# Second FFN of a decoder trunk: weight-block sums for six up tiles made in HBM ahead, and the second up part wholly by seven block products

## The chip, the cores and the metric

The kernel runs on one core of one Trainium2 chip. The metric is device time in microseconds for one launch; lower is better. TensorE (PE) multiplies, VectorE (DVE) and ScalarE (ACT) do the elementwise work, GpSimd (POOL) does a little elementwise work and issues DMAs that add into HBM, SyncE (SP) issues nearly all loads.

## The reference

A two-layer decoder trunk on 512 positions of width 1024, all in float32. The part that matters here is the gated FFN that stands in both layers:

```python
def conv_ffn(xn, w_up, conv_w, conv_b, w_down):          # d = 1024, D_FF = 2816
    S = xn.shape[1]
    h = xn @ w_up                                         # 1024 -> 2 * 2816
    hp = jnp.pad(h, ((0, 0), (CONV_WIDTH - 1, 0), (0, 0)))
    c = conv_b + sum(hp[:, t:t + S] * conv_w[t] for t in range(CONV_WIDTH))
    g, u = jnp.split(c, 2, axis=-1)
    return (jax.nn.silu(g) * u) @ w_down
```

Layer 0 is a gMLP mixer, this FFN and a gated embedding; then one shared K/V projection; layer 1 is windowed attention, the FFN again and a gated embedding; a final RMSNorm ends it.

## The kernel before

**Splits.** Every float32 matrix product is made of three products of float32r parts: an operand is cast to float32r (`wh`, by ACT) and the remainder is taken (`wl`, by DVE), and PE adds high x high, high x low and low x high. So each weight block that PE uses has first cost one ACT cast and one DVE subtraction. They are made in `pump`, in pieces called units of up to 1024 columns, into four pairs of buffers (`WBUFS = 4`), so at most four units ahead of PE.

**Up tiles.** The up projection is cut into 22 tiles (index 0 to 21; "11th to 16th" are 10 to 15). Tile j makes 128 gate rows and the 128 line rows that belong to them. A plain tile (`up`) takes 8 blocks of the inner dimension, 2 halves and 3 products: 48 matmuls of 512 columns, and 2 units of weights. A tile in `UPS` is made by `woven_up`: the 2x2 block product with seven block multiplications instead of eight (Strassen's, in Winograd's form), each for 4 pairs of blocks: 7 x 4 x 3 = 84 matmuls of 256 columns. It needs sums of weight blocks. With the four blocks 0 to 3 of a pair, `weave` makes on DVE block 1 + block 0 and block 1 + block 3 (one instruction of 1024 columns, L163), then the next two sums from these (512 columns each, L164 and L165). The blocks and sums make three and a half units (three of 1024 columns and one of 512), each cast and subtracted in `pump`. After the products `woven_up` puts the two results together with two more DVE instructions (L812, 256 columns; L813, 512 columns) and five small ACT copies. Its output lies in SBUF: in the tiles `gate` and `line`, or, for the tiles in `ASIDE`, in a slot of the activations named `out`.

**After a tile**, `gated` applies the convolution (one ACT instruction and two DVE instructions of about 512 columns, L762, on each half), silu (ACT) and the product (DVE, L769). Two tiles that follow each other are one `Pair`, whose block sums and splits (L518 to L535, L312) feed the down projection.

**Parts.** The 22 tiles go in three parts (0 to 7, 8 to 15, 16 to 21), and the first tile of the next part is computed ahead of the down projection of the part before. The second part thus runs on PE as: tiles 9 to 15, then tile 16, then the down projection of tiles 8 to 15 in `woven_add` (PE tiles `dx` and `dy`, sums of weights in `weave` too), whose results GpSimd's queue adds into HBM (`saved<-head`, `saved<-tail`, L600). In the second part of both FFNs the tiles 9, 10, 12, 14 and 16 are woven and 11, 13 and 15 are plain.

**Loads.** `load` fetches one piece (one tile's weights, 1 MB) by one DMA on SP's queue into the next of three staging slots; a woven tile takes a second slot for its sums. A slot is free when the last split that reads it is done.

**Order.** Each engine works through its instructions in the order in which the scheduler of the framework left them. `behind(a, b)` only holds a after b in that order; it makes no wait.

Of the kernel before, what the change touches and what calls it, by code (L numbers as in the profile page):

```python
# [52 lines left out]
def tile_yoco(ctx: ExitStack, tc: tile.TileContext, t, out: bass.AP, out_b: bass.AP):  # L53
    nc = tc.nc
# [9 lines left out]
    dram = ctx.enter_context(tc.tile_pool(name="dram", bufs=1, space=bass.MemoryType.DRAM))  # L64
# [3 lines left out]
        return mmp.tile([P, S], F32, tag="mm", name=name)  # L68


    pieces, paired, woven, beside = [], set(), set(), set()

    def plan(ap_, n, cols, own=None):
# [23 lines left out]
    def plan_woven(w, n_chunks, k0, k1):  # L97

        for c in range(n_chunks):
            n = (k1 - k0) * P  # L100
            woven.add(len(pieces))
            pieces.append((w[c, :, k0 * 256 : k1 * 256], 2 * n, [(0, n)] * 3 + [(0, n // 2)], None))

    def plan_ups(l, j0, j1):
        for j in range(j0, j1):
            (plan_woven if j in UPS else plan_cols)(t["w_up"][l, j : j + 1], 1, *((0, KD) if j in UPS else (KD,)))

    def plan_ffn(l):
        plan(t["pT"][l], 2 * S, S, own=[(mp, "m4", "m5")])
# [33 lines left out]
    def behind(ins, front):  # L143

        tc.add_manual_dep(ins.ins, front.ins.name,
                          mybir.DependencyInfo(mybir.DependencyClass.NoSync, mybir.DependencyReason.DATA),
                          reason="order")

    def staged(name):
        tags = state["tags"]  # L150
        r = wp.tile([P, 2 * UNIT], F32, tag=f"r{tags[state['turn'] % len(tags)]}", bufs=1, name=name)
        state["turn"] += 1
        return r

    def weave(i, q):


        n = pieces[i][1] // 4
        g = raws[i][:, : 4 * n].rearrange("p (k b m) -> p b k m", b=4, m=P)
        if q == 0:  # L160
            s = sums[i] = staged(f"wsum{i}")[:, : 4 * n].rearrange("p (b k m) -> p b k m", b=4, m=P)
            k = n // P
            nc.vector.tensor_add(s[:, 0::3], g[:, 1:2].to_broadcast([P, 2, k, P]), g[:, 0::3])  # L163
            nc.vector.tensor_add(s[:, 2], s[:, 3], g[:, 0])  # L164
            nc.vector.tensor_add(s[:, 1], s[:, 2], g[:, 2])  # L165
        return (g[:, 0:3:2], sums[i][:, 2:4], sums[i][:, 0:2], g[:, 3:4])[q]

    def load(upto, queue=nc.sync):
        while state["raw"] < min(upto, len(pieces)):
            j = state["raw"]  # L170
            a, m = pieces[j][:2]
            r = raws[j - 1][:, UNIT:] if j in beside else staged(f"wraw{j}")
            ins = queue.dma_start(r[:, :m].rearrange("p (c m) -> p c m", c=2) if j in paired else r[:, :m], a)
            for front in state["sent"].pop(j, []):
                behind(ins, front)
            raws[j] = r
            state["raw"] += 1
# [145 lines left out]
    class Norm:  # L323
# [11 lines left out]
        def square(self, k, eng=None):  # L335
            sq = tp.tile([P, S], F32, tag="sq", name=f"{self.name}sq{k}")
            box["squared", k] = ins = nc.scalar.activation(sq, h[k], AF.Square)
            if self.acc is None:
                self.acc = sq
            else:  # L340
                acc = tp.tile([P, S], F32, tag="acc", name=f"{self.name}acc{k}")
                self.added = (eng or nc.gpsimd).tensor_add(acc, self.acc, sq)
                self.acc = acc
            return ins

# [99 lines left out]
        def rstd(self):  # L445

            r = tp.tile([P, S], F32, tag="rstd", name=f"{self.name}rstd")
            if self.line is not None:
                nc.gpsimd.dma_start(r, self.line.partition_broadcast(P))
            else:  # L450
                nc.scalar.copy(r, self.spread(0, S // 64))
            return r

    def inv_root(ms, name, scale=1.0, n=None):
        if n is None:
            n = ms.shape[1]
            ms = [(slice(None), ms)]
        m = const.tile([P, n], F32, tag=f"ms{n}", bufs=2, name=f"{name}m")
        for some, x in ms:
            box["m"] = nc.vector.tensor_scalar(m[some, :], x, scale, EPS, op0=ALU.mult, op1=ALU.add)  # L460
        r = const.tile([P, n], F32, tag=f"rt{n}", bufs=2, name=f"{name}rt")
        nc.gpsimd.tensor_tensor(r, m, minus_half[:, :n], op=ALU.pow)
        return r

    box = {}
# [264 lines left out]
    def ffn(l, norm, nxt):  # L730
# [4 lines left out]
            behind(nc.sync.dma_start(saved[k], h[k]), box["squared", k])  # L735

        def up(j, later=False):
            if j in UPS:
# [13 lines left out]
            return pss if later else gated(j, pss)  # L752
# [34 lines left out]
        def woven_up(j, later):  # L787

            product = products(ins)
            n = PAIRS * P  # L790
            chain, other = psum(f"ux{j}")[:, first], psum(f"uy{j}")
            if j in ASIDE:
                head, tail = couple(ASIDE[j], f"out{j}", F32)
# [18 lines left out]
            nc.vector.tensor_sub(tail[:, second], tail[:, second], side)  # L812
            nc.vector.tensor_add(head, head, other)  # L813
            return (head, tail) if later else gated(j, (head, tail))
# [91 lines left out]
    def ple(l, norm, nxt, pe):  # L906
        xs = norm.xs[0][0]
        rstd, held = None, []
        for c in range(4):
            parts = chunk(256, KD)  # L910
# [114 lines left out]
    edge = at.tile([P, PAIRS, 2, N], F32R, tag="vtl", name="edge")  # L1025
    us = [Pair(c, edge, f"us{c}", range(3 * PAIRS)) for c in range(PAIRS)]
    for c in range(4):
        parts = chunk(256, KD)
        ups = [psum(f"u{c}_{j}") for j in range(2)]
        for j in range(2):  # L1030
# [47 lines left out]
    for k in range(KD):  # L1078
        nm.split(k, 1)
        if k == 3:  # L1080
            nm.turn()
    rt = nm.begin(rows=2)

    state["tags"] = [0, 1]
    parts = chunk(256, KD)
# [1 line left out]
    mm3(qps[0], parts, xq, 0)  # L1087
    rstd = nm.rstd()
    mm3(qps[1], parts, xq, P)

    for j in range(2):
        kf = tp.tile([P, S], F32, tag="acc", name=f"kf{j}")
# [314 lines left out]
    r = [f"r{(state['turn'] + j) % 3}" for j in range(3)]  # L1407
# [229 lines left out]
```

## Time and profile before

| | us |
|---|---|
| median of 3 runs | 1100.43 (1099.83 to 1101.02) |
| the profiled execution's own time | 1100.39 |
| its span | 1098.7 |
| second FFN, tile 9 to the down projection of part two | 838.6 to 922.7 of the span |
| first FFN, the same stretch | 290.8 to 373.5 of the span |

The profile is of one execution; times inside it count from the span's start. 1.69 us of the execution's time lie outside the span. A busy PE in the profile is a PE without gaps between matmuls; the chain of waits tells what PE was held by, and the timeline of DVE when each split was ready. In the timeline an instruction's duration overlaps the next one's start by about 0.08 us, so what an instruction costs its engine is read from start to start.

### The profile page before, as it was taken

Reading aid. Unit: us, or ns where it says so; the run is one execution under the profiler, and the core shown is the slowest. Engines: PE = TensorE matmul, PEld = TensorE weight load, DVE = VectorE, ACT = ScalarE, POOL = GpSimd, SP = SyncE. Lnnn points to the kernel's source line nnn. Section 1 sums busy time; section 2 is a strip of 40 time slices with the busy share of each in tenths; the row PEclk is TensorE's granted clock in tenths of the full one; section 3 lists DMA queues with packets and bytes.
Section 4 is the critical chain, followed back from the end, with each engine's and each line's share of the span. In section 5 each row is a group of like instructions: output and inputs, shape, how many; then the busy total and the mean of one; then the engine's idle time right before and its main releaser. Section 6 shows DMA issues by size and latency. Waiting matters only on the chain.

```text
span 1098.7 us, 17476 instructions
## 1 busy us (share of the span) xinstructions
PE 1089.1 (99%) x6629; PEld 974.4 (89%) x6629; DVE 959.0 (87%) x1540; ACT 661.0 (60%) x1141; POOL 125.0 (11%) x192
## 2 busy tenths in 40 slices
PE   9999999999999999999999999999999999999997
PEld 7888988899998999988888887888999989999886
DVE  5588889999899989877988997799998999898887
ACT  5735666565676656655656775565655666567544
POOL 2200200000100010021114452000001000100200
PEclk9999999999999999999999999999999999999999
DMA  9621674125633267353234216441255333664534
GB/s 317 113 88 39 178 264 150 43 77 116 155 115 116 79 160 222 120 190 112 67 87 135 78 58 227 176 153 39 77 142 128 115 116 86 156 220 142 203 95 98
DMA packets 47508, 144.24 MB, mean 131 GB/s; under 512 B 13048, under 2 KB 18688, under 8 KB 36928
## 3 DMA queue, kind: packets, MB, share of 16 engines
q1 hardware_dynamic: 40560, 128.77, 35.6%
q0 software_dynamic: 5296, 9.70, 6.7%
q10 hardware_dynamic: 1568, 4.65, 1.1%
q8 instruction: 52, 0.85, 0.3%
q14 instruction: 32, 0.26, 0.1%
HBM read 116.89 MB, written 18.88 MB: 124 GB/s over the span
## 4 chain that ended last, share of the span: by engine, by line
PE 95%; DVE 2%; issue 1%; ACT 1%; DMA 0%; SPq 0%; POOLq 0%; POOL 0%; ACTq 0%
PE up L234 20%; PE ux L234 10%; PE dx L234 10%; PE uy L234 8%; PE dy L234 8%; PE d L234 6%; PE q L234 4%; PE gate L234 4%; PE u L234 4%; PE o L234 4%; PE up L750 2%; PE pv L1326 1%; PE v L244 1%; PE v L245 1%; PE v L246 1%; PE pin L234 1%
## 5 line engine op out<-in xcount | busy, mean ns | idle before, releaser
L204 DVE TENSOR_TENSOR wl<-wraw,wh 128x1024 fp32r<-128x1024 f32 (+2 forms) x198 | 217.3, 1102 | 42.8 <-ACT wh L203 41.9
L203 ACT CAST wh<-wraw 128x1024 fp32r<-128x1024 f32 (+2 forms) x197 | 182.8, 933 | 107.6 <-PE up L234 21.8
L203 ACT CAST wh<-wsum 128x1024 fp32r<-128x1024 f32 x84 | 88.3, 1052 | 62.7 <-issue 14.9
L204 DVE TENSOR_TENSOR wl<-wsum,wh 128x1024 fp32r<-128x1024 f32 x84 | 102.5, 1225 | 16.1 <-ACT wh L203 16.0
L762 DVE SCALAR_TENSOR_TENSOR c<-up,vec,c 128x511 f32<-128x511 f32 (+1 forms) x88 | 65.0, 744 | 2.4 <-ACT c L760 1.9
L234 PE MATMUL up<-nf10h,wh 128*128 128x512 f32 x160 | 62.3, 389 | 0.0
L234 PE MATMUL up<-nf00h,wh 128*128 128x512 f32 x160 | 62.3, 389 | 0.0
L234 PE MATMUL up<-nf10l,wh 128*128 128x512 f32 x160 | 62.3, 389 | 0.0
L234 PE MATMUL up<-nf00l,wh 128*128 128x512 f32 x160 | 62.3, 389 | 0.0
L234 PE MATMUL up<-nf00h,wl 128*128 128x512 f32 x160 | 62.1, 389 | 0.0
L234 PE MATMUL up<-nf10h,wl 128*128 128x512 f32 x160 | 62.0, 389 | 0.0
L600 POOL DMA_DIRECT2D saved<-head x16 | 13.9, 871 | 412.9 <-DVE head L720 412.9
L760 ACT ACTIVATE c<-up,vec 128x512 f32<-128x512 f32 x44 | 34.0, 777 | 31.8 <-PE up L234 26.6
L163 DVE TENSOR_TENSOR wsum<-wraw 128x1024 f32<-128x1024 f32 x42 | 51.2, 1220 | 0.6
L234 PE MATMUL ux<-t,wh 128*128 128x256 f32 x264 | 50.4, 283 | 0.0
L234 PEld LDWEIGHTS ux<-t,wh 128*128 128x128 f32 x264 | 41.2, 192 | 0.0
L234 PE MATMUL ux<-t,wl 128*128 128x256 f32 x132 | 37.4, 283 | 0.0
L234 PEld LDWEIGHTS up<-nf00h,wl 128*128 128x128 f32 x160 | 30.0, 188 | 6.2
L234 PEld LDWEIGHTS up<-nf10h,wl 128*128 128x128 f32 x160 | 30.0, 188 | 6.2
L234 PEld LDWEIGHTS up<-nf00l,wh 128*128 128x128 f32 x160 | 30.0, 188 | 6.2
L234 PEld LDWEIGHTS up<-nf10l,wh 128*128 128x128 f32 x160 | 30.0, 188 | 6.2
L234 PEld LDWEIGHTS up<-nf10h,wh 128*128 128x128 f32 x160 | 30.0, 188 | 6.0
(769 smaller groups left out, 3734.3 us busy)
## 6 DMA issues: line engine op xcount, KB each, us to landing
wraw<-in_w_up SPq DMA_DIRECT2D x44, 1024.0 KB, 5.6
wraw<-in_w_down SPq DMA_DIRECT2D x16, 1024.0 KB, 5.0
wraw<-in_w_gate SPq DMA_DIRECT2D x8, 1024.0 KB, 5.5
wraw<-in_w_down SPq DMA_DIRECT2D x8, 768.0 KB, 4.5
wraw<-in_w_u SPq DMA_DIRECT2D x4, 1024.0 KB, 9.4
wraw<-in_w_out SPq DMA_DIRECT2D x4, 1024.0 KB, 4.9
saved<-head POOLq DMA_DIRECT2D x16, 256.0 KB, 4.2
saved<-tail POOLq DMA_DIRECT2D x16, 256.0 KB, 4.1
```

The costliest lines, as they stand in the source:

```text
L163: nc.vector.tensor_add(s[:, 0::3], g[:, 1:2].to_broadcast([P, 2, k, P]), g[:, 0::3])
L203: cast = nc.scalar.copy(hi, src)
L204: state["split"] = splits[u] = cast, nc.vector.tensor_sub(low, src, hi.bitcast(F32))
L234: return [nc.tensor.matmul(ps, w, x, start=first and j == 0, stop=last and j == len(todo) - 1, skip_group_check=onto) for j, (w, x) in enu ...
L244: nc.tensor.matmul(ps, xh[:, s], wh[:, a:b], start=st, stop=False)
L245: nc.tensor.matmul(ps, xl[:, s], wh[:, a:b], start=False, stop=False)
L246: nc.tensor.matmul(ps, xh[:, s], wl[:, a:b], start=False, stop=en)
L600: box["onto"] = nc.gpsimd.dma_start(x, y, accum_op=ALU.add)
L750: nc.tensor.matmul(ps, w[:, off + s * P : off + (s + 1) * P], x, start=k == 0 and x is xh and w is wh, stop=k == KD - 1 and x is xl)
L760: nc.scalar.activation(c, ps, AF.Identity, bias=v("conv_b", l * 2 * NJ + col), scale=cw[2])
L762: ins = nc.vector.scalar_tensor_tensor(c[:, tap:], ps[:, : S - tap], cw[2 - tap], c[:, tap:], op0=ALU.mult, op1=ALU.add)
L1326: nc.tensor.matmul(ps, lhs, rhs, start=j == 0, stop=j == len(todo) - 1)
```

## The change

It touches the up tiles 10 to 15 of the second FFN.

1. **Plain to woven.** Tiles 11, 13 and 15 of the second FFN become woven, so that in its second part all of 9 to 16 are. Their outputs go to slots 7, 12 and 12 (`ASIDE`).
2. **Sums in HBM.** For tiles 10 to 15 of the second FFN `weave` makes no sums any more. They are made in HBM during the first FFN, in two batches (tiles 10 and 11, tiles 12 to 15). Each batch is six steps: SP copies block 1 twice into the sums' places; GpSimd's queue adds block 3 to the one and block 0 to the other; copies the first sum on; adds block 0; copies on; adds block 2. Rows are runs of 128 floats in the steps that read the weights. The steps are called at the first FFN's tiles 1, 2, 3 and 5 (first batch) and 9, 10, 11 and 13 (second batch); each is held in its queue's order behind the last load (SP) or behind the last instruction marked `box["onto"]` (GpSimd).
3. **Loads.** Such a tile is loaded by four DMAs on SP's queue into two slots (the blocks 0 and 2 and two sums into `wraw`, two sums and block 3 into `wsum`): 1.75 MB in place of 1 MB. Around the six tiles `flip` changes the order of two slots.

```diff
-UPS = (7, 8, 9, 10, 12, 14, 16, 17, 18, 20, 21)
-ASIDE = {7: 12, 9: 7, 17: 7, 20: 6}
+UPS = [(7, 8, 9, 10, 12, 14, 16, 17, 18, 20, 21), (7, 8, 9, 10, 11, 12, 13, 14, 15, 16, 17, 18, 20, 21)]
+ASIDE = [{7: 12, 9: 7, 17: 7, 20: 6}, {7: 12, 9: 7, 11: 7, 13: 12, 15: 12, 17: 7, 20: 6}]
+BATCHES = [
+    (1, 10, 12, [("up", 0, 1), ("up", 0, 2), ("up", 0, 3), ("up", 0, 3), ("up", 0, 5), ("up", 0, 5)]),
+    (1, 12, 16, [("up", 0, 9), ("up", 0, 10), ("up", 0, 11), ("up", 0, 11), ("up", 0, 13), ("up", 0, 13)]),
+]
...
+    def sums_ahead(l, j0, j1, keys):
+        n = KD // 2 * P
+        whole = dram.tile([(j1 - j0) * P, 4 * n], F32, name=f"sums{l}_{j0}")
+        w = t["w_up"][l, j0:j1].rearrange("j p (k b m) -> (j p) k b m", b=4, m=P)
+        s = {x: whole[:, i * n : (i + 1) * n].rearrange("r (k m) -> r k m", m=P) for i, x in enumerate((2, 3, 0, 1))}
...
+        def copy(x, y):
+            behind(nc.sync.dma_start(x, y), state["loaded"])
+        def onto(x, y):
+            behind(nc.gpsimd.dma_start(x, y, accum_op=ALU.add), box["onto"])
+        def then(x, y):
+            behind(nc.gpsimd.dma_start(s[x], s[y]), box["onto"])
+        steps = [lambda: [copy(s[x], w[:, :, 1]) for x in (3, 0)],
+                 lambda: [onto(s[x], w[:, :, x]) for x in (3, 0)],
+                 lambda: then(2, 3), lambda: onto(s[2], w[:, :, 0]),
+                 lambda: then(1, 2), lambda: onto(s[1], w[:, :, 2])]
...
@@ in weave
+        if i in summed:
+            a, c = raws[i]
+            return (a[:, : 2 * n].rearrange("p (k b m) -> p b k m", b=2, m=P),
+                    a[:, 2 * n :].rearrange("p (b k m) -> p b k m", b=2, m=P),
+                    c[:, : 2 * n].rearrange("p (b k m) -> p b k m", b=2, m=P),
+                    c[:, 2 * n : 3 * n].rearrange("p (b k m) -> p b k m", b=1, m=P))[q]
@@ in load
+            if j in summed:
+                n = m // 4
+                if j - 1 not in summed:
+                    flip()
+                x, y = raws[j] = staged(f"wraw{j}"), staged(f"wsum{j}")
+                for there, here in ((x[:, : 2 * n].rearrange("p (k m) -> p k m", m=P),
+                                     a.rearrange("p (k m) -> p k m", m=P)[:, 0::2]),
+                                    (x[:, 2 * n :], summed[j][:, : 2 * n]),
+                                    (y[:, : 2 * n], summed[j][:, 2 * n :]),
+                                    (y[:, 2 * n : 3 * n].rearrange("p (k m) -> p k m", m=P),
+                                     a.rearrange("p (k m) -> p k m", m=P)[:, 3::4])):
+                    state["loaded"] = queue.dma_start(there, here)
+                state["raw"] += 1
+                if j + 1 not in summed:
+                    flip()
+                continue
```

**What moves in the engines' order.** Three places. On **DVE**, around the end of tile 10 of the second FFN (`wl221` to `wl224` are splits of tiles 11 and 12, `line10` and `gate10` put tile 10's result together, `act1_0_2l` is a split of activations). Before:

```order
L204 TENSOR_TENSOR wl221_9150<-wraw85_9117,wh221_9149 128x1024
L312 TENSOR_TENSOR act1_0_2l_9072<-act1_0u_9073,act1_0_2h_9071 128x512
L163 TENSOR_TENSOR wsum86_9182<-wraw86_9178 128x2x512
L204 TENSOR_TENSOR wl222_9181<-wraw86_9178,wh222_9180 128x1024
L164 TENSOR_TENSOR wsum86_9182<-wsum86_9182,wraw86_9178 128x512
L812 TENSOR_TENSOR line10_9086<-line10_9086,side10_9087 128x256
L165 TENSOR_TENSOR wsum86_9182<-wsum86_9182,wraw86_9178 128x512
L813 TENSOR_TENSOR gate10_9085<-gate10_9085,uy10_9084 128x512
L204 TENSOR_TENSOR wl223_9219<-wsum86_9182,wh223_9218 128x1024
```

Now:

```order
L274 TENSOR_TENSOR wl221_9172<-wraw85_9135,wh221_9171 128x1024
L382 TENSOR_TENSOR act1_0_2l_9090<-act1_0u_9091,act1_0_2h_9089 128x512
L885 TENSOR_TENSOR line10_9104<-line10_9104,side10_9105 128x256
L886 TENSOR_TENSOR gate10_9103<-gate10_9103,uy10_9102 128x512
L274 TENSOR_TENSOR wl222_9201<-wsum85_9136,wh222_9200 128x1024
L274 TENSOR_TENSOR wl223_9240<-wsum85_9136,wh223_9239 128x512
L835 SCALAR_TENSOR_TENSOR c10_0_9219<-gate10_9103,vec_86,c10_0_9219 128x511
```

Tile 12's three sums are gone; tile 11 has four splits (`wl220` to `wl223`) where it had two, so `wl222` and `wl223`, before the first of tile 12, are now the last of tile 11.

On **DVE** again, the last rows before the first split of the down projection (`wl238` before, `wl244` now; `c15` and `a15` are tile 15's convolution and gate, `wsum91` the down projection's sums, `act1_3` the last pair). Before:

```order
L762 SCALAR_TENSOR_TENSOR c15_1_9715<-up15_1_9662,vec_84,c15_1_9715 128x511
L163 TENSOR_TENSOR wsum91_9777<-wraw91_9773 128x2x512
L762 SCALAR_TENSOR_TENSOR c15_1_9715<-up15_1_9662,vec_84,c15_1_9715 128x510
L164 TENSOR_TENSOR wsum91_9777<-wsum91_9777,wraw91_9773 128x512
L769 TENSOR_TENSOR a15_9719<-a15_9719,c15_1_9715 128x512
L165 TENSOR_TENSOR wsum91_9777<-wsum91_9777,wraw91_9773 128x512
L532 TENSOR_TENSOR act1_3t_9654<-a15_9719,a14_9650 128x256
L533 SCALAR_TENSOR_TENSOR act1_3u_9725<-act1_3t_9654,a15_9719 128x256
L312 TENSOR_TENSOR act1_3_0_9722<-a15_9719,act1_3_0_9722 128x512
L535 SCALAR_TENSOR_TENSOR act1_3u_9725<-act1_3u_9725,a15_9719 128x256
L204 TENSOR_TENSOR wl238_9776<-wraw91_9773,wh238_9775 128x1024
```

Now:

```order
L835 SCALAR_TENSOR_TENSOR c15_0_9905<-out15_9790,vec_86,c15_0_9905 128x510
L216 TENSOR_TENSOR wsum91_9967<-wraw91_9963 128x2x512
L842 TENSOR_TENSOR a15_9913<-a15_9913,c15_1_9909 128x512
L217 TENSOR_TENSOR wsum91_9967<-wsum91_9967,wraw91_9963 128x512
L604 TENSOR_TENSOR act1_3t_9785<-a15_9913,a14_9781 128x256
L605 SCALAR_TENSOR_TENSOR act1_3u_9919<-act1_3t_9785,a15_9913 128x256
L382 TENSOR_TENSOR act1_3_0_9916<-a15_9913,act1_3_0_9916 128x512
L607 SCALAR_TENSOR_TENSOR act1_3u_9919<-act1_3u_9919,a15_9913 128x256
L218 TENSOR_TENSOR wsum91_9967<-wsum91_9967,wraw91_9963 128x512
L382 TENSOR_TENSOR act1_3_1_9917<-act1_3t_9785,act1_3_1_9917 128x512
L382 TENSOR_TENSOR act1_3_2_9918<-act1_3u_9919,act1_3_2_9918 128x512
L274 TENSOR_TENSOR wl244_9966<-wraw91_9963,wh244_9965 128x1024
```

All three splits of the last pair now stand ahead of the first split of the down projection; before, two of them stood behind it. All four convolution instructions of tile 15 now come after that tile's last product; before, the two of its first half came earlier.

On **POOL**, between the first FFN's two down projections (`saved<-head` and `saved<-tail` are their results). Before:

```order
L600 DMA saved0_5_1548<-tail2_2805 128x512
L600 DMA saved0_6_1549<-head3_2923 128x512
L600 DMA saved0_7_1550<-tail3_2924 128x512
L600 DMA saved0_0_1543<-head0_3980 128x512
L600 DMA saved0_1_1544<-tail0_3981 128x512
```

Now:

```order
L672 DMA saved0_6_1551<-head3_2933 128x512
L672 DMA saved0_7_1552<-tail3_2934 128x512
L130 DMA sums1_12_85<-in_w_up 512x4x128 x2
L133 DMA sums1_12_85<-sums1_12_85 512x512
L130 DMA sums1_12_85<-in_w_up 512x4x128
L133 DMA sums1_12_85<-sums1_12_85 512x512
L130 DMA sums1_12_85<-in_w_up 512x4x128
L672 DMA saved0_0_1545<-head0_3998 128x512
L672 DMA saved0_1_1546<-tail0_3999 128x512
```

The second batch's six DMAs stand between the two down projections; from the third on, each waits for the one whose sum it reads. The first batch's six stand in the same way ahead of the first FFN's first down projection.

More of the change, by code (lines that the diff above doesn't have):

```diff
@@ L68, in psum, with behind @@
         return mmp.tile([P, S], F32, tag="mm", name=name)
+    def behind(ins, front):
+        tc.add_manual_dep(ins.ins, front.ins.name,
+                          mybir.DependencyInfo(mybir.DependencyClass.NoSync, mybir.DependencyReason.DATA),
+                          reason="order")
     pieces, paired, woven, beside = [], set(), set(), set()
@@ L102, in plan_woven, with come @@
             pieces.append((w[c, :, k0 * 256 : k1 * 256], 2 * n, [(0, n)] * 3 + [(0, n // 2)], None))
+    summed, far_sums, to_come = {}, {}, {}
+    def sums_ahead(l, j0, j1, keys):
[3 more added lines that the diff above has]
+        s = {x: whole[:, i * n : (i + 1) * n].rearrange("r (k m) -> r k m", m=P) for i, x in enumerate((2, 3, 0, 1))}
+        for j in range(j0, j1):
+            far_sums[l, j] = whole[(j - j0) * P : (j - j0 + 1) * P]
+        def copy(x, y):
[8 more added lines that the diff above has]
+                 lambda: then(1, 2), lambda: onto(s[1], w[:, :, 2])]
+        for key, step in zip(keys, steps):
+            to_come.setdefault(key, []).append(step)
+    def come(*key):
+        for step in to_come.pop(key, []):
+            step()
+    for batch in BATCHES:
+        sums_ahead(*batch)
     def plan_ups(l, j0, j1):
         for j in range(j0, j1):
-            (plan_woven if j in UPS else plan_cols)(t["w_up"][l, j : j + 1], 1, *((0, KD) if j in UPS else (KD,)))
+            if (l, j) in far_sums:
+                summed[len(pieces)] = far_sums[l, j]
+            (plan_woven if j in UPS[l] else plan_cols)(t["w_up"][l, j : j + 1], 1,
+                                                       *((0, KD) if j in UPS[l] else (KD,)))
     def plan_ffn(l):
@@ L141, in tile_yoco, with flip @@
     state = {"raw": 0, "unit": 0, "next": 0, "tags": [0, 1, 2], "turn": 2, "pt": 0, "sent": {}}
[L143 to L147, printed above, removed]
+    def flip():
+        tags, i = state["tags"], state["turn"] + 1
+        a, c = i % 3, (i + 1) % 3
+        tags[a], tags[c] = tags[c], tags[a]
     def staged(name):
@@ L448, in rstd @@
             if self.line is not None:
-                nc.gpsimd.dma_start(r, self.line.partition_broadcast(P))
+                box["onto"] = nc.gpsimd.dma_start(r, self.line.partition_broadcast(P))
             else:
@@ L737, in up @@
         def up(j, later=False):
-            if j in UPS:
+            come("up", l, j)
+            if j in UPS[l]:
                 return woven_up(j, later)
@@ L791, in woven_up @@
             chain, other = psum(f"ux{j}")[:, first], psum(f"uy{j}")
-            if j in ASIDE:
-                head, tail = couple(ASIDE[j], f"out{j}", F32)
+            if j in ASIDE[l]:
+                head, tail = couple(ASIDE[l][j], f"out{j}", F32)
             else:
@@ L909, in ple @@
         for c in range(4):
+            come("gate", l, c)
             parts = chunk(256, KD)
@@ L1027, in tile_yoco @@
     for c in range(4):
+        come("u", c)
         parts = chunk(256, KD)
@@ L1082, in tile_yoco @@
     rt = nm.begin(rows=2)
+    come("k")
     state["tags"] = [0, 1]
@@ L1089, in tile_yoco @@
     mm3(qps[1], parts, xq, P)
+    come("q")
     for j in range(2):
@@ L1406, in tile_yoco @@
     parts2 = chunk(S, KD, ahead=2 * WBUFS)
-    r = [f"r{(state['turn'] + j) % 3}" for j in range(3)]
+    r = [f"r{state['tags'][(state['turn'] + j) % 3]}" for j in range(3)]
     turned_b = squares(wp, r[0], "turned_b")
```

5 lines of the change are left out of this document (4 added, 1 removed).

## The prediction

> **What bounds the kernel now.** The page first. PE is busy for 99% of the span and is 95% of the chain that ended last; DVE is busy for 87%.
>
> ```profile
> span 1098.7 us, 17476 instructions
> PE 1089.1 (99%) x6629; PEld 974.4 (89%) x6629; DVE 959.0 (87%) x1540; ACT 661.0 (60%) x1141; POOL 125.0 (11%) x192
> PE 95%; DVE 2%; issue 1%; ACT 1%; DMA 0%; SPq 0%; POOLq 0%; POOL 0%; ACTq 0%
> ```
>
> Shares are means, so next the busy times by stretch: the second FFN's part two, a piece of it from the first split of tile 11 to that of the down projection, and the first FFN's part two.
>
> ```profile
> core 0: us, PE busy (x) PEld busy (x) DVE busy (x) ACT busy (x) POOL busy (x), PEclk, DMA share, GB/s
> 838.60:922.70 84.10, 84.10 (x570) 77.67 (x569) 80.98 (x118) 55.43 (x89) 1.34 (x2) 1.00 0.34 108
> 853.75:920.24 66.49, 66.49 (x424) 60.16 (x424) 64.81 (x97) 43.55 (x69) 0.00 (x0) 1.00 0.30 104
> 290.80:373.50 82.70, 82.70 (x559) 76.27 (x558) 79.58 (x116) 54.40 (x89) 1.32 (x2) 1.00 0.34 110
> ```
>
> PE has no gap at all in the stretch that the change shortens, but DVE is busy for 81.0 of its 84.1 us. PE sets the end by a small margin; the question is what DVE does when PE gets shorter.
>
> **PE: three tiles become shorter.** The chain in order of time gives both kinds of tile:
>
> ```profile
> 869.97 1.43 PE ux L234 x12
> ...
> 880.03 10.91 PE up L234 x48
> 890.94 1.43 PE ux L234 x12
> ```
>
> Tile 12 (woven) starts at 869.97 and tile 13 (plain) at 880.03: 10.06 us. Tile 13 takes 10.91. A tile that changes kind saves 0.85 us, three save 2.55 us. That is all that PE can gain, since it has no gap there to close.
>
> **DVE: what goes and what comes.** One stretch of its timeline, tile 10's end, prices each kind of instruction from start to start:
>
> ```profile
> 861.71 0.41 DVE L812 TENSOR_TENSOR line<-line,side 128x256 f32<-128x256 f32 x1
> 862.05 0.68 DVE L165 TENSOR_TENSOR wsum<-wsum,wraw 128x512 f32<-128x512 f32 x1
> 862.65 0.68 DVE L813 TENSOR_TENSOR gate<-gate,uy 128x512 f32<-128x512 f32 x1
> 863.25 1.21 DVE L204 TENSOR_TENSOR wl<-wsum,wh 128x1024 fp32r<-128x1024 f32 x1
> 864.39 0.75 DVE L762 SCALAR_TENSOR_TENSOR c<-gate,vec,c 128x511 f32<-128x511 f32 x1
> 865.06 0.74 DVE L762 SCALAR_TENSOR_TENSOR c<-line,vec,c 128x511 f32<-128x511 f32 x1
> ```
>
> 256 columns cost 0.34 us, 512 cost 0.60, 1024 cost 1.14, a convolution step 0.67. The sums of a tile (1024, 512, 512) are 2.34 us; tiles 10, 12 and 14 lose them: -7.0. A tile that becomes woven has one more split of 1024 and one of 512 (1.74) and two instructions to put it together (0.94): 2.68, three times +8.0. So DVE has 1.0 us more to do while PE has 2.55 us less, against some 3 us in which DVE is idle in that stretch. All of those would have to be usable.
>
> **Where the two meet.** PE's next fixed point is the down projection's first use of a remainder, and DVE makes that remainder at the end of a long run without free choice of order:
>
> ```profile
> 847.44 0.69 DVE L813 TENSOR_TENSOR out9h<-out9h,uy 128x512 f32<-128x512 f32 x1 [0.47 <-PE uy L234]
> ...
> 853.75 1.22 DVE L204 TENSOR_TENSOR wl<-wraw,wh 128x1024 fp32r<-128x1024 f32 x1
> ...
> 871.37 1.52 DVE L762 SCALAR_TENSOR_TENSOR c<-up,vec,c 128x511 f32<-128x511 f32 x2
> 872.99 0.69 DVE L769 TENSOR_TENSOR a<-a,c 128x512 f32<-128x512 f32 x1
> ...
> 891.41 0.69 DVE L204 TENSOR_TENSOR wl<-wraw,wh 128x512 fp32r<-128x512 f32 x1 [0.43 <-ACT wh L203]
> ...
> 912.55 0.69 DVE L204 TENSOR_TENSOR wl<-wraw,wh 128x512 fp32r<-128x512 f32 x1 [0.73 <-ACT wh L203]
> ...
> 919.10 1.22 DVE L204 TENSOR_TENSOR wl<-wraw,wh 128x1024 fp32r<-128x1024 f32 x1
> ```
>
> ```profile
> 922.60 0.28 PE L234 MATMUL dx<-edge,wl 128*128 128x256 f32 x1
> ```
>
> Now the remainder is ready at 919.10 + 1.14 = 920.24 and PE takes it up at 922.60: it lies 2.36 us early. If PE never waited in the changed kernel it would be there 2.55 us sooner, at 920.05.
>
> DVE starts tile 11's first split at 853.75, right behind tile 9's results; those hang on PE (DVE waits 0.47 us for it at 847.44), not on tile 10's sums, so I keep this start. In the order of before, 95 instructions stand from there to the down projection's first split: 20 of 1024 columns, 30 of 512, 21 of 256 and 24 convolution steps, or 22.8 + 18.0 + 7.1 + 16.0 = 63.9 us. The trace shows 66.49, so 2.6 us were waits. In the order of after there are 103: 21, 34, 24 and 24. (Of the extra instructions two come from the split of the down projection now standing behind all splits of the last pair.) That is 23.9 + 20.4 + 8.2 + 16.0 = 68.5 us, so the remainder is ready at 922.25 at the earliest, later than 920.05.
>
> To this come waits. Below they can't go under zero; above I take the 2.6 us of before. The two of 0.43 and 0.73 us were waits for ACT's cast, which waited for a buffer that PE still read: a DVE that is behind does not meet these. What stays are steps that read the result of the one before: two convolution steps of one half and the product took 872.99 - 871.37 = 1.62 us and not 1.33, so 0.3 us; in the new order tiles 11 and 13 have this. I take 0.75 us, near those 0.6. So the remainder comes at 923.0, PE has waited there for about 3 us, and stands 0.4 us later than at 922.60 now. What PE saved it waits for.
>
> Behind this point DVE has fewer instructions for each block of the down projection than PE needs time (four splits, three sums, two small steps: 4.0 + 2.3 + 0.9 us against some 10), so nothing more is lost, but a loss stays.
>
> **ACT** gets 1.5 casts and five copies for each new woven tile, about 3.5 us by its rows here (1049 ns for a cast of 1024 columns, 385 for a copy):
>
> ```profile
> L203 ACT CAST wh<-wraw 128x1024 fp32r<-128x1024 f32 x11 | 11.5, 1049 | 5.3 <-PE uy L234 2.9 <-issue 1.4 <-ACT line L556 1.0
> L556 ACT ACTIVATE line<-ux 128x256 f32<-128x256 f32 x7 | 2.7, 385 | 1.4 <-PE ux L234 1.4
> ```
>
> That makes 55.4 + 10.5 = 66 of 82 us: ACT has time left, and I cost it at nothing.
>
> **The sums in the first FFN.** No row shows an accumulation from HBM to HBM. The queues' totals bound it:
>
> ```profile
> q1 hardware_dynamic: 40560, 128.77, 35.6%
> q0 software_dynamic: 5296, 9.70, 6.7%
> ...
> saved<-head POOLq DMA_DIRECT2D x16, 256.0 KB, 4.2
> ```
>
> The columns are packets, MB and share. q1 is SP's: 35.6% of 16 engines' span is 6258 engine-us, 48.6 for a MB. **The four loads** of a summed tile in the second FFN (1.75 MB for 1 MB, on SP's queue one behind the other) take 5.6 us of all 16 engines instead of 3.2, beside 10 us of PE's work on the tile before. That hides them, so they cost nothing; without that cover each us late is one more us that DVE waits, up to the 2.6 us taken as the upper end.
>
> q0 is GpSimd's: 6.7% of 16 engines' span is 1178 engine-us, 121 for a MB or 0.222 for a packet. A step of the second batch moves 1.05 MB in 2048 runs: 8 us of all 16 engines by bytes, 28 us by packets. I take the lower end: most of q0's packets are additions of 2 KB rows. Behind the six DMAs on POOL's queue stands the second down projection's first `saved<-head`:
>
> ```profile
> 382.71 0.86 POOL L600 DMA_DIRECT2D saved<-head  x1 [89.86 <-DVE head L720]
> ```
>
> POOL had waited for 89.9 us before it, which is the room for the six: 15 us for each. With 8 us and the 4.2 us from issue to landing of a 256 KB one, six in a row take at most 73 us. Cost nothing. The Trainium skill (DMA: Bandwidth & Descriptors, Anatomy of one DMA) puts a DMA of this queue at 2.0 us and its bytes at 436 GB/s; that is an estimate of 4.4 us for a step, also nothing on the path, but the row of 4.2 us for a quarter of the bytes is already above it, so I stay with the row.
>
> **The sum.** The profiled execution took 1100.39 us, 1.69 of them outside the span, within 0.04 of the median. -2.55 on PE, +2.95 waited at the down projection, and 0.1 for loads of the first FFN beside the sums: 1100.9. With waits from 0 to 2.6 us this case runs from 1100.0 to 1102.7. About 0.2%, 2.2 us, is what a measurement of this kernel can tell from no change; the case lies almost wholly within it. Chance 0.55.
>
> **Rivals.**
>
> *PE keeps all of it (0.15).* Tile 10's sums, 2.34 us, also leave DVE, ahead of 853.75. If that start moves forward by as much, the remainder is ready at 919.9 and PE waits for little: 1100.4 - 2.55 = 1097.9. For it: DVE's high load just there. Against it: the wait at 847.44, where DVE had time over and stood for PE.
>
> *The sums slow the first FFN's loads (0.25).* There DVE is as full (79.6 of 82.7 us), and a woven tile's sums start as soon as its load is there:
>
> ```profile
> 303.14 0.33 SPq L173 DMA_DIRECT2D wraw<-in_w_up  x1
> ```
>
> ```profile
> DMA to landing us min/median/max: 4.8/5.1/7.4
> ```
>
> ```profile
> 311.02 1.22 DVE L163 TENSOR_TENSOR wsum<-wraw 128x1024 f32<-128x1024 f32 x1
> ```
>
> The loads between 260 and 320 us land after 4.8 to 7.4 us, tile 12's thus at about 308.2, 2.8 us before use. Shared evenly with additions it needs twice its 3.2 us and lands 3 us later: nothing is lost. If a step takes the 28 us of the count by packets, a load stands behind more than its like. Late by L, tiles 12 and 14 make DVE wait 2 x (L - 2.8); its 3.1 us of idle time and a lead of 2.4 as in the second FFN cover 5.5. So it decides from L = 5.5 on, and at 7.3 PE loses 3.5: with the 0.4 of the likeliest case 1104.3. For it: the 7.4 us belong to a stretch in which GpSimd's queue adds its 256 KB results. Against it: DMA is 34% busy there. The Trainium skill (DMA: Bandwidth & Descriptors, Issuing engines are not separate DMA queues) says that DMAs of all queues run on the same 16 engines and interleave: by this rule another queue is no shelter, and the 7.4 us agree.
>
> *GpSimd's queue is late (0.05).* Above 15 us a step, `saved<-head` at 382.71 starts late and the buffers of the down projection's results don't come free: at 28 us for each of four additions some 40 us late, of which two buffers, one every 10 us, cover 20: 1120.
>
> **The numbers.** Forecast 1100.9. Faster by over 0.2%: 0.15, the first rival. Slower by over 0.2%: most of the second, the third, and the upper edge of the forecast: 0.29. Within: 0.56. From 1098.0 to 1104.5 leaves out the last rival and edges.
>
> **What would show it.** Right: PE's tiles 11, 13 and 15 of 84 matmuls in about 10.05 us each; a PE wait of 2 to 4 us at the first `dx` with `wl`, ended by DVE; DVE without idle time from tile 11 on. Wrong: no such wait (then DVE had more slack than its rows say), or waits of DVE for `wraw` between 300 and 350 us, or a late `saved<-head` at 383.

## The result, and the profile after

| | us |
|---|---|
| before, median of 18 runs | 1100.43 (1099.47 to 1101.45) |
| after, median of 18 runs | 1102.45 (1101.39 to 1104.46) |
| ratio after / before | 1.0019, 95% interval 1.0012 to 1.0026 |
| the profiled execution of after, its span | 1101.82, 1100.1 |

The forecast was 1100.9 with a range from 1098.0 to 1104.5. The time lies in the range, 1.5 us above the forecast: 2.0 us slower than before, where the forecast had 0.5. The profiled execution of after is one of its faster ones, 1.43 us longer than the profiled one of before.

The head of the page of after (span, busy times, the chain that ended last by engine):

```profile
span 1100.1 us, 17783 instructions
PE 1088.6 (99%) x6737; PEld 979.1 (89%) x6737; DVE 959.5 (87%) x1543; ACT 669.5 (61%) x1162; POOL 142.9 (13%) x204
PE 88%; DVE 5%; SPq 2%; issue 2%; DMA 1%; ACT 1%; POOL 0%; POOLq 0%; DVEq 0%; ACTq 0%
```

PE's share of the chain went from 95% to 88%, DVE's from 2% to 5%, and SP's queue and DMA, 0% before, have 2% and 1%. Now the stretch of the change, from the same point of tile 9 to the down projection's first use of a remainder; first before, then after:

```profile
core 0: us, PE busy (x) PEld busy (x) DVE busy (x) ACT busy (x) POOL busy (x), PEclk, DMA share, GB/s
845.93:922.60 76.67, 76.67 (x508) 70.34 (x508) 74.07 (x109) 50.49 (x80) 0.00 (x0) 1.00 0.29 97
```

```profile
845.75:923.36 77.61, 75.61 (x617) 74.07 (x616) 75.96 (x114) 60.06 (x103) 0.00 (x0) 1.00 0.50 160
853.57:923.22 69.65, 67.79 (x551) 66.25 (x550) 68.93 (x104) 54.32 (x93) 0.00 (x0) 1.00 0.46 148
```

The stretch is 0.94 us longer. The second row of after is DVE's queue from tile 11's first split to the down projection's; DVE is busy for 68.93 of its 69.65 us. What PE's weight loads waited for in the second FFN's part two (total, times, longest), before, then after:

```profile
PEld uy L234 <- ACT side L805: 0.7, 2, 0.3
```

```profile
PEld uy L304 <- ACT side L878: 1.2, 1, 1.2
PEld dx L304 <- DVE wl L274: 1.2, 1, 1.2
PEld ux L304 <- ACT out L872: 0.3, 2, 0.2
PEld ux L304 <- ACT line L628: 0.2, 1, 0.2
PEld ux L304 <- ACT out11h L872: 0.2, 1, 0.2
```

The two long ones in the timeline:

```profile
920.68 0.19 PEld L304 LDWEIGHTS uy<-nf10h,wh 128*128 128x128 f32 x1 [1.21 <-ACT side L878]
...
923.36 0.19 PEld L304 LDWEIGHTS dx<-edge,wl 128*128 128x128 f32 x1 [1.19 <-DVE wl L274]
```

Two waits of 1.2 us and some of 0.2. The second long one is the one that was forecast: DVE makes the remainder at the end of its queue, without a pause:

```profile
920.28 0.68 DVE L218 TENSOR_TENSOR wsum<-wsum,wraw 128x512 f32<-128x512 f32 x1
920.88 0.68 DVE L382 TENSOR_TENSOR act<-act_3t,act 128x512 fp32r<-128x512 f32 x1
921.49 0.68 DVE L382 TENSOR_TENSOR act<-act_3u,act 128x512 fp32r<-128x512 f32 x1
922.09 1.21 DVE L274 TENSOR_TENSOR wl<-wraw,wh 128x1024 fp32r<-128x1024 f32 x1
```

The first long one is DVE's lateness too, but ACT passes it on. ACT's copy `side`, which PE waits for, stands in ACT's order behind the silu `a` and a cast of tile 15, and those wait for DVE:

```profile
916.51 0.63 ACT L841 ACTIVATE a<-c 128x512 f32<-128x512 f32 x1 [1.11 <-DVE c L835]
...
918.18 0.62 ACT L381 CAST act<-a 128x512 fp32r<-128x512 f32 x1 [0.25 <-DVE a L842]
918.79 1.05 ACT L273 CAST wh<-wsum 128x1024 fp32r<-128x1024 f32 x1
919.75 0.61 ACT L381 CAST act<-act_3t 128x512 fp32r<-128x512 f32 x1
920.26 0.36 ACT L878 COPY side<-uy 128x256 f32<-128x256 f32 x1
```

### The profile page after: what moved, and what is told of

Same layout as the page of the kernel before. It is cut to its first block, busy times and chain, and to the rows that moved or that the text cites. A ratio compares the mean times of both kernels' runs of the same rounds, so it can differ in the third digit from the quotient of the medians.

```text
span 1100.1 us, 17783 instructions
## 1 busy us (share of the span) xinstructions
PE 1088.6 (99%) x6737; PEld 979.1 (89%) x6737; DVE 959.5 (87%) x1543; ACT 669.5 (61%) x1162; POOL 142.9 (13%) x204
## 3 DMA queue, kind: packets, MB, share of 16 engines
q0 software_dynamic: 18544, 19.14, 12.2%
## 4 chain that ended last, share of the span: by engine, by line
PE 88%; DVE 5%; SPq 2%; issue 2%; DMA 1%; ACT 1%; POOL 0%; POOLq 0%; DVEq 0%; ACTq 0%
PE up L304 17%; PE ux L304 11%; PE dx L304 10%; PE uy L304 9%; PE dy L304 8%; PE q L304 4%; PE gate L304 4%; PE u L304 4%; PE o L304 4%; PE d L304 4%; PE up L823 2%; SPq L1471 2%; DMA wraw<-in_w_gate 1%; PE pv L1403 1%; PE v L314 1%
## 5 line engine op out<-in xcount | busy, mean ns | idle before, releaser
L273 ACT CAST wh<-wraw 128x1024 fp32r<-128x1024 f32 (+2 forms) x197 | 184.1, 939 | 105.9 <-PE up L304 17.3
L273 ACT CAST wh<-wsum 128x1024 fp32r<-128x1024 f32 x90 | 92.0, 1022 | 61.7 <-PE uy L304 17.7
L835 DVE SCALAR_TENSOR_TENSOR c<-up,vec,c 128x511 f32<-128x511 f32 (+1 forms) x76 | 56.1, 744 | 2.4 <-ACT c L833 2.0
L304 PE MATMUL ux<-t,wh 128*128 128x256 f32 x300 | 57.7, 285 | 0.0
L304 PEld LDWEIGHTS ux<-t,wh 128*128 128x128 f32 x300 | 46.7, 192 | 0.8 <-ACT out L872 0.3
L304 PE MATMUL up<-nf10h,wh 128*128 128x512 f32 x112 | 43.6, 389 | 0.0
L304 PE MATMUL up<-nf10l,wh 128*128 128x512 f32 x112 | 43.6, 389 | 0.0
L304 PE MATMUL up<-nf10h,wl 128*128 128x512 f32 x112 | 43.3, 389 | 0.0
L304 PE MATMUL ux<-t,wl 128*128 128x256 f32 x150 | 42.5, 283 | 0.0
L841 ACT ACTIVATE a<-c 128x512 f32<-128x512 f32 x44 | 27.8, 631 | 17.3 <-DVE c L835 17.3
L304 PEld LDWEIGHTS up<-nf00h,wh 128*128 128x128 f32 x160 | 30.0, 188 | 6.0
L304 PE MATMUL uy<-nf10h,wh 128*128 128x256 f32 x112 | 32.8, 293 | 1.2 <-ACT side L878 1.0
```

The source lines that it names most:

```text
L273: cast = nc.scalar.copy(hi, src)
L304: return [nc.tensor.matmul(ps, w, x, start=first and j == 0, stop=last and j == len(todo) - 1, skip_group_check=onto) for j, (w, x) in enu ...
L835: ins = nc.vector.scalar_tensor_tensor(c[:, tap:], ps[:, : S - tap], cw[2 - tap], c[:, tap:], op0=ALU.mult, op1=ALU.add)
L841: box["silu"] = nc.scalar.activation(a, cs[0], AF.Silu)
```

## The experiments

Three theories. **DVE's queue:** what PE saves it waits for, because DVE cannot be sooner at the down projection's first remainder. **Transfers (rival 1):** the sums in HBM or the four loads cost the time. **ACT's copies (rival 2):** woven tiles in a row make PE wait for ACT, whatever DVE does.

The table has all timed runs. "Stretch" is the time in the trace from the first `dx` with `wl` in the second FFN's part one to that in its part two, less the 124.00 us of before (-: PE's order there is another). A before of the same set is the kernel before, timed beside that run; c2 is a single execution, e3 has two, all others eleven or more. "Gate loads" is issue to landing of the last three loads of gate weights near the end, added up; it is used further below.

| run | time | before, same set | stretch | gate loads |
|---|---|---|---|---|
| before | | | 0 | 16.6 |
| after | 1102.45 | 1100.43 | +0.95 | 17.0 |
| e1_made_unused | 1100.45 | 1100.43 | -0.02 | 16.6 |
| e2_sums_only | 1100.46 | 1100.43 | +0.19 | 16.5 |
| e3_woven_only | 1112.77 | 1100.43 | - | 17.0 |
| e4_sums_to_16 | 1102.03 | 1100.43 | -1.28 | 17.3 |
| c1_after_again | 1102.33 | 1100.71 | +0.93 | 17.4 |
| e5_order | 1101.25 | 1100.71 | -0.22 | 17.2 |
| e8_sixteen_later | 1100.28 | 1100.71 | -1.28 | 17.7 |
| e9_later_order | 1100.78 | 1100.71 | - | 17.2 |
| e10_copy_first | 1099.74 | 1100.31 | -1.95 | 17.5 |
| c2_before_again | 1099.74 | 1100.31 | -0.01 | 16.5 |

### e1: the sums made, but not used

```diff
-UPS = [(7, 8, 9, 10, 12, 14, 16, ...), (7, 8, 9, 10, 11, 12, 13, 14, 15, 16, ...)]
+UPS = [(7, 8, 9, 10, 12, 14, 16, ...)] * 2        # ASIDE in the same way
-            if (l, j) in far_sums:
+            if False:
```

> Tiles 11, 13 and 15 plain and all sums on DVE again, as before the change; the sums in HBM are still made during the first FFN, but nobody loads them. Theory (DVE's queue eats what PE saves): the transfers hide, 1100.4 us, within 0.6. Rival 1 (the transfers or what they do to other loads cost the time): about 1102.4. Rival 2 (woven tiles in a row make PE wait for ACT's copies, whatever DVE has to do): 1100.4 as well, so this run speaks only on rival 1.

Measured 1100.45 us, ratio 1.0000 (0.9992 to 1.0009). The transfers alone cost nothing that can be measured. They are not free of effect: in the profile of after, where the same sums are made, the loads of weights between 295 and 350 us took longer (issue to landing, first before, then after):

```profile
DMA to landing us min/median/max: 4.8/4.9/5.1
```

```profile
DMA to landing us min/median/max: 5.1/8.2/9.9
```

### e2: the sums used by the tiles that were woven already

```diff
-            if (l, j) in far_sums:
+            if (l, j) in far_sums and j in UPS[l]:     # UPS and ASIDE as in e1
```

> Tiles 11, 13 and 15 plain; tiles 10, 12 and 14 take their sums from HBM by four loads. DVE loses 7.0 us of sums in the second FFN, PE does what it did before. Theory: PE had no wait there, so nothing is gained: 1100.4 us, within 0.6, with DVE some 4.7 to 7 us early or idle at the down projection's first remainder. Rival 1 (the sums or the four loads cost the time): 1102.4. Rival 2: 1100.4.

Measured 1100.46 us, ratio 1.0000 (0.9991 to 1.0009). DVE loses 7.0 us of sums, 4.7 of them in this stretch (those of tiles 12 and 14; tile 10's come ahead of it), and PE gains nothing. DVE is busy for 3.8 us less (70.27 us against 74.07), and by as much more it waits for ACT's casts (5.7 us, before 2.0):

```profile
845.96:922.82 76.86, 76.86 (x509) 70.26 (x509) 70.27 (x103) 50.16 (x80) 0.00 (x0) 1.00 0.39 130
```

```profile
DVE wl L274 <- ACT wh L273: 5.7, 7, 1.3
```

Against the 1102.45 of after, e1 and e2 show that rival 1 as it was put does not hold: neither the transfers nor the four loads cost the 2 us. e2 has the four loads of only three tiles, and a DVE with time to spare; that those of all six cost nothing is read from after, where DVE waited for none of them.

### e3: the woven tiles with their sums on DVE

```diff
-BATCHES = [ (1, 10, 12, ...), (1, 12, 16, ...) ]
+BATCHES = []
```

> Tiles 11, 13 and 15 woven, but all sums on DVE, nothing made in HBM. Theory: five tiles' sums of 2.34 us, 11.7 us, come into DVE's stretch between tile 11's first split and the down projection's; DVE waits there 1.4 us now, so PE comes 10.3 to 11.7 us later: 1112.8 to 1114.2 us. Rival 1 (the transfers cost the time): the 2.55 us of PE without them, about 1098. Rival 2 (ACT's copies): as after the change, 1102.4.

Measured 1112.77 us (2 runs), just under the lower edge of the theory's 1112.8 to 1114.2; rival 1 said 1098, rival 2 1102.4. Five tiles' sums on DVE cost PE 10.3 us more than after: on this stretch each further microsecond of DVE is nearly one of PE.

### e4: tile 16's sums in HBM too

```diff
-    (1, 12, 16, [("up", 0, 9), ...
+    (1, 12, 17, [("up", 0, 9), ...
```

> As after the change, and tile 16's sums made in HBM too. DVE has 2.34 us less ahead of the down projection's first remainder. Theory: PE's two waits (1.17 and 1.15 us) go nearly whole, 1100.1 to 1100.6 us, and what stays against PE's own saving are the short waits of 0.1 to 0.2 us for ACT's copies. Rival 1: 1102.5 or more (a quarter more of transfers). Rival 2: the wait of 1.17 us for ACT's copy and the short ones stay, only the other shrinks: 1101.3.

Measured 1102.03 us (1100.53 to 1104.81): expected 1100.1 to 1100.6, a miss as a whole, but made of two parts that the trace keeps apart. In the second FFN it went as the theory says: the stretch is 2.23 us shorter than after, the wait for the split is gone and the one for `side` shrank to 0.3. In the first FFN PE lost 3.75 us (250.72 to 378.46 us between the two parts' first `dx` with `wl`, 127.74 against 123.99). The loads there, the two waits that matter, and PE's clock behind them:

```profile
DMA to landing us min/median/max: 5.0/8.9/11.9
```

```profile
DVE wsum L216 <- DMA wraw<-in_w_up: 2.1, 1, 2.1
PEld ux L304 <- ACT gate L876: 1.9, 1, 1.9
```

```profile
330.50:333.80 3.30, 3.30 (x18) 3.30 (x17) 3.30 (x4) 1.55 (x3) 0.00 (x0) 0.50 1.41 170
334.00:337.00 3.00, 3.00 (x21) 2.73 (x20) 2.17 (x4) 1.44 (x2) 0.00 (x0) 1.00 1.36 161
```

With a quarter more to add, the load of tile 12 lands 10.1 us after its issue, DVE waits 2.1 us for it and stays late; ACT waits 2.0 us for DVE's product just ahead of its copy, and PE waits 1.9 us for the copy. Then the granted clock is 0.50 for the 3.3 us of the row above, which is worth about 1.65 us (an estimate: half of 3.3). This is the prediction's second rival, which the batch of the change escapes.

### c1: the changed kernel again

> The changed kernel unaltered, as the measure for the other runs of this set and for a second profile of it. Theory: again two PE waits of together 2 to 2.6 us around the down projection's first remainder in the second FFN, and nothing lost in the first FFN: 1102.0 to 1102.9 us. Rival (late loads in the first FFN, in some executions): those two waits smaller in this profile than in the first, or a PE wait between 300 and 350 us.

Measured 1102.33 us, ratio 1.0018 (1.0009 to 1.0027). The two waits are 1.25 and 1.19 us, the stretch +0.93, and between 300 and 350 us PE has only the wait of 0.3 us that stands in before too.

### e5: three DVE instructions behind the down projection's first split

```diff
...                                                    # names for the three instructions
                 u = state["next"]
+                if (l, i) == (1, 1):
+                    for x in (pair.made[1][1], pair.made[2][1], sumins[units[u][0]]):
+                        behind(x, splits[u][1])
                 woven_add(...)
```

> The changed kernel with three DVE instructions (two splits of the last pair, 0.60 us each, and the last weight sum, 0.60 us) ordered behind the down projection's first split. DVE has as much work, but that split comes 1.8 us sooner. Theory: the wait of 1.15 us for the split goes; the wait of 1.17 us for ACT's copy, just ahead of it, stays, since tile 15's product on DVE comes no sooner: 1101.1 to 1101.6 us. Rival (the time is lost by ACT or by transfers, the waits at the split only make up for PE being early): 1102.4.

Measured 1101.25 us, 1.08 less than the changed kernel in the same set, as expected. The wait for the split is gone, that for `side` is what it was:

```profile
PEld uy L304 <- ACT side L879: 1.2, 1, 1.2
PEld ux L304 <- ACT out L873: 0.3, 2, 0.2
```

DVE did as much work as before this edit; only the place of the split in its queue changed. So it is the queue up to that point that PE waited for.

### e8: tile 16's sums as a batch of their own, later

```diff
     (1, 12, 16, [...]),
+    (1, 16, 17, [("up", 0, 17), ("up", 0, 18), ("up", 0, 19), ("up", 0, 19), ("up", 0, 21), ("up", 0, 21)]),
```

> Tile 16's sums made in HBM as well, but as a batch of their own in the first FFN's third part, so that the second batch keeps the size it has in the changed kernel. Theory: the second FFN is as short as with the larger batch (1.3 us shorter than before the change, by the trace of that run) and the first FFN loses nothing: 1099.1 us, within 0.5. Rival 1 (any more of such transfers costs the time, wherever they are): 1102. Rival 2 (ACT's copies hold PE whatever DVE does): 1101.3.

Measured 1100.28 us, 2.05 less than the changed kernel and 0.43 less than before (ratio 0.9997, 0.9988 to 1.0006). The traces answer each half of e4: the same stretch, -1.28, and nothing lost in the first FFN (124.00 us where e4 had 127.74). The total is 1.2 us above what was expected (a range of 0.5 was given), so as a forecast of the time it is a miss. Part of that rest lies outside the span: in all executions of e8, e9 and e10 the time is 2.09 to 2.26 us longer than the span, in all other runs 1.65 to 1.84. These three kernels have a third batch; why it costs 0.4 us there was not looked into. For the remainder see the tail below.

### e9: e8 with e5's order

> The one before, and the three DVE instructions ordered behind the down projection's first split. Theory: with tile 16's sums gone DVE is no longer late at that split, so the order is worth at most the 0.3 us of wait that is left: 1098.8 to 1099.4 us, the same as without it. If DVE were still the bound there: 1.2 to 1.8 us less than without it.

Measured 1100.78 us: no gain over e8 (1100.28), as the theory says, though above the range given; its time has the 0.4 us outside the span too, and in its profile PE loses 0.5 us in the first FFN and has waits of 0.5 and 0.3 us in the last down projection, neither in the place of the edit. There the wait for `side` is replaced by one of 0.2 us for the split.

### e10: ACT's copy ahead of the convolution

```diff
...                                                    # box["conv"] is ACT's convolution instruction
-            behind(box["silu"], nc.scalar.copy(head[:, first], chain))
+            mark = nc.scalar.copy(head[:, first], chain)
+            behind(box["silu"], mark)
+            if l and 11 <= j <= 15:
+                behind(box["conv"], mark)              # on top of e8
```

> The version with tile 16's sums as a batch of their own, and in the second FFN's tiles 11 to 15 ACT's first copy of a woven tile's result ordered ahead of the second convolution instruction of the tile before it (and the silu behind it). Theory (the short PE waits of 0.22 us ahead of ux come from that order): three of them go, 0.7 us; DVE, with 0.3 us to spare at the down projection, may wait up to 0.3 us more for each of those convolutions. So 0 to 0.7 us less than without the order: 1099.6 to 1100.3 us against 1100.3. Rival (these short waits belong to woven tiles whatever the order): they stay at 0.22 us in the trace.

Measured 1099.74 us against 1100.31 before (ratio 0.9996, 0.9987 to 1.0005). All short waits ahead of `ux` are gone and the stretch is 0.67 us shorter than in e8; only this is left of PE's waits there:

```profile
PEld uy L305 <- ACT side L882: 0.3, 1, 0.3
```

So the short waits ahead of `ux` belonged to ACT's order, not to woven tiles as such. This rests on the stretch; the time is only 0.14 us better than e8's, each against its own before. It is the shortest version tried, 2.2 us below the changed kernel (c1), again each against its own before; from the kernel before it cannot be told apart.

### c2: the kernel before again, and the tail

> The kernel before, unaltered, for a second profile of it. In the traces so far the last PE matmul comes 41.0 us after the last load of gate weights has landed, and the last three of those loads took 16.5 to 16.7 us together in the three kernels with plain tiles 11, 13 and 15, 17.0 to 17.7 us in the seven with woven ones. If that belongs to the kernels: 16.4 to 16.8 us here. If it is chance from run to run: anything from 16.4 to 17.7.

Gate loads 16.5 us, in the range of the kernels with plain tiles. The chain of waits of after, in order of time near its end, shows what these loads do:

```profile
1026.18 4.80 DMA wraw<-in_w_gate
1033.94 5.56 DMA wraw<-in_w_gate
1043.02 2.26 DVE wl L274
1045.35 5.89 DMA wraw<-in_w_gate
```

The last wait of PE there, before and after:

```profile
PEld np1ms L388 <- DVE np1quarter L379: 0.4, 1, 0.4
```

```profile
PEld np1ms L460 <- DVE np1quarter L451: 0.6, 1, 0.6
```

In all twelve traces the last matmul of PE comes 40.96 to 41.08 us after the last of these loads has landed (41.30 in e2). So near the end PE hangs on a chain of loads, each issued when a split has freed its buffer. What ties PE to the last one is the wait above: ACT casts what it brings, in ACT's order ahead of an instruction that DVE's `np1quarter` needs. Where ACT waited for this load, PE goes on 4.82 to 4.90 us after the landing; in e2, the one trace where ACT did not, 5.12 us after.

In the four traces with plain tiles 11, 13 and 15 the three loads took 16.5 to 16.6 us, in the eight with woven ones 17.0 to 17.7. Not all of that reaches the end: from the issue of the first of the three to the landing of the last it is 24.6 to 25.0 us with plain tiles and 25.0 to 26.0 with woven ones: 25.1 in after, 25.3 to 25.4 in c1, e5 and e10, 26.0 in e8. For these five that is 0.2 to 1.1 us more than before's 24.8. After, c1, e5, e8 and e10 are 0.7 to 1.4 us above what their stretch says; without the 0.4 us outside the span of e8 and e10 it is 0.4 to 1.1. The size is the same, but run by run the two do not match, so the loads are a part of the rest and not shown to be all of it. Why these loads take longer was not found: the last two are 272 packets each, of the same median time, in before as in after. A part of the rest may also lie in the first FFN: a wait of 0.4 to 0.7 us at 372.4 to 375.5 us stands in five of the nine profiles with the sums in HBM, in none of the three without.

## Why the prediction came out as it did

- **PE's saving, -2.55: right.** 144 matmuls of 512 columns became 252 of 256; at the steps seen in the traces (227.3 and 119.4 ns) that is -2.64.
- **DVE as the bound at the first remainder: right.** The start of tile 11's first split stayed (853.57, with everything 0.18 sooner), the remainder was ready at 923.22 where 923.0 was forecast. The waits in DVE's queue were 1.4 us in place of 0.75, the work 68.3 in place of 68.5. Its lateness cost PE 2.3 us (forecast 2.95), half of it one step earlier, through ACT's copy `side`; so the wait at the first `dx` with `wl` alone was 1.2 us, where 2 to 4 had been named as the sign. e3 and e5 show the queue as the cause by adding and by moving work, e4 and e8 by taking some away.
- **ACT at nothing: this step failed, by 1.3 us.** ACT had 16 us to spare in the sum, but its order put the copies that free PE's accumulator behind two convolution instructions of the tile before:

```profile
860.10 0.81 ACT L833 ACTIVATE c<-gate,vec 128x512 f32<-128x512 f32 x1
860.81 0.81 ACT L833 ACTIVATE c<-line,vec 128x512 f32<-128x512 f32 x1
861.51 0.36 ACT L872 COPY out11h<-ux 128x256 f32<-128x256 f32 x1
```

```profile
861.92 0.30 PEld L304 LDWEIGHTS ux<-t,wh 128*128 128x128 f32 x2 [0.16 <-ACT out11h L872]
```

  Such a wait costs PE 0.22 us, with the slower step of the matmul behind it. All small gaps between PE's matmuls in the stretch add up to 1.86 us, before to 0.60. These +1.26, the -2.64 and the +2.32 give the +0.94 of the stretch; the forecast had +0.40. e10 takes 0.67 us of it away by order alone. The other 0.6 us stands at ACT's copies as well, but no run tested what would remove it.
- **The four loads at nothing: right.** They landed in 3.9 to 8.8 us and DVE waited for none of them.
- **GpSimd's queue: right.** The second batch's six DMAs ran from 292.60 to 354.76 us, 62 us where at most 73 was forecast, and the next result was added without delay:

```profile
340.94 2.30 POOL L130 DMA_DIRECT2D sums<-in_w_up  x1 [6.57 <-DMA sums<-sums]
382.62 0.87 POOL L672 DMA_DIRECT2D saved<-head  x1 [39.37 <-DVE head L792]
```

  The Trainium skill (DMA: Bandwidth & Descriptors, Anatomy of one DMA) gave an estimate of 4.4 us for such a step; the additions took 12.4 to 19.6 us from issue to landing here, the copies 6.5 and 14.5. The measurement decides: the additions are 2.8 to 4.5 times as long. (The row of 4.2 us, which the prediction calls already above the estimate, is below 4.4; it is above what the same working gives for its own quarter of the bytes, 2.6, an estimate too.) Each addition also took longer than the prediction's own 12.2 us a step (8 + 4.2). The total held because the first two ran side by side and one copy was short.
- **The first FFN's loads, +0.1: right in size.** Tile 12's load landed 7.4 us after its issue and tile 13's 9.9. DVE waited 1.8 us for loads, which the prediction had named as a sign of being wrong, but PE waited no longer than in before (0.7 us in both): between the two parts' first `dx` with `wl` are 124.01 us, before 123.99. The rival that this belongs to was right that loads come late, and wrong on when it costs: it had PE lose nothing up to 5.5 us of lateness and 3.5 us at 7.3. In e4 tile 12's load is 5.2 us later than in before, and PE loses 3.75 us: 1.9 in a wait and about 1.65 at half the clock, which was no term of the rival. That 3.75 is near 3.5 is luck.
- **The end of the kernel as a fixed distance behind the second FFN: not in the sum.** The chain of loads of gate weights took 0.2 us longer in after and 0.5 in its repeat. With the 0.94 and 0.93 of the stretch this makes 1.2 of the 2.0 us measured, and 1.4 of 1.6. The cause of the longer loads stays open, and so does the remainder.
- **The total: in part luck.** The wait for DVE was priced 0.6 us too high and ACT's 1.3 us were not in the sum; these partly cancel. That the change stays within 2.2 us of before is by 0.2 us only.

## What to carry to other kernels

When two engines are both over 95% busy on a stretch, shortening one is worth only what the other has to spare, and that is counted instruction by instruction up to the next point where they meet. An engine with time to spare can still hold the others by its order: look at what stands in its queue ahead of the copies that free an accumulator. Extra transfers were free here with four tiles in a batch and not with five, when a load beside them came later than its lead; so size the batch by that lead, not by the mean load of DMA.

## What the hardware showed beyond what was expected

After waits of PE the granted clock can fall to half for some microseconds. In e4 a wait of 1.93 us was followed by 3.4 us at 0.50 (above). In e3 it was 6.8 us at 0.50, twice as long, from 884.05 to 890.88 us. That began 1.4 us after the end of a wait of 3.37 us, and one of 1.19 us fell into it; the first row below is the part behind the second wait. Behind a wait of 3.0 us the clock stayed (second row):

```profile
885.50:890.90 5.40, 5.40 (x26) 5.40 (x27) 5.40 (x8) 2.83 (x4) 0.00 (x0) 0.50 0.43 135
...
922.90:926.00 3.10, 3.10 (x26) 3.10 (x27) 3.10 (x5) 1.31 (x3) 0.00 (x0) 1.00 0.00 0
```

In after, two waits of 1.2 us within 3 us had no such effect. The Trainium skill (TensorE: Matmul & The Clock Gate, Part 1) says that the clock is halved after an idle window of about 3.4 us; e4 disagrees, since 1.93 us was enough there.
